# Attention with its tokens in natural order: neighbour values by tokens, the other heads' blocks by stride

## The chip, the cores and the metric

The kernel runs on one core of a Trainium2 chip. The metric is the device time of one execution in microseconds. A core has a matrix engine (TensorE, PE in the profile; PEld is its weight load), a vector engine (VectorE, DVE), an activation engine (ScalarE, ACT), a general engine (GpSimd, POOL) and a queue engine (SyncE, SP). Operands lie in SBUF, 128 partitions wide; matmul results go to PSUM, eight banks of 128 x 512 fp32.

## The reference

Two residual layers over 512 tokens of 1024 features, each a mixer and a SwiGLU block with a norm ahead; layer 0 mixes by causal pooling, layer 1 by attention, and a last norm ends it. The change lies in the attention mixer, which has 16 heads of 64 features in three groups:

```python
ATTN_PATTERNS = ((128, 1), (512, 4), (2048, 16))      # window, dilation
...
qkv = jnp.einsum('bsd,de->bse', h, w_qkv).reshape(B, S, 3, N_HEADS, HEAD_DIM)
q = rope(qkv[:, :, 0]) * HEAD_DIM ** -0.5
k = rope(qkv[:, :, 1])
v = qkv[:, :, 2]
for (window, dilation), n_g in zip(ATTN_PATTERNS, HEAD_GROUPS):    # 6, 5, 5 heads
    o_g, lse_g = dilated_window_attention(q[:, :, sl], k[:, :, sl], v[:, :, sl], window, dilation)
```

The first six heads ("neighbour heads") look at the last 128 tokens, dilation 1: their blocks are 128 consecutive tokens, and a block sees itself and the block before. The other ten ("far heads") have dilations of 4 and 16: a query sees only keys whose token number has the same remainder by 4 (or by 16), so the kernel gives them four blocks by residue, block r holding the tokens 4j + r. The groups' outputs are weighted by a softmax over their log-sum-exps and go through an output projection.

## The kernel before

All products are fp32 by splitting: every operand is a high part rounded for the matrix engine and a low rest, and a product is three matmuls, high-high, high-low and low-high. Weights are loaded by DMA into `wraw`, cast to the high part on ACT (L171), subtracted on DVE for the low part (L175), and kept in a ring of five pairs (`wspl`). `queue` lists them in the order of use; `weights(i)` loads five items ahead and splits four ahead, and its argument `held` counts earlier items that are still in use. TensorE's instructions run in the order in which the program writes them; the other engines' orders are planned from priorities and dependencies, and `high_priority(URGENT)` moves an instruction ahead.

The operand of attention, `h`, is the normed and turned stream: features on partitions, tokens along the row, in a high and a low part. Before the change its 512 tokens stand in residue order: first the tokens 0, 4, 8, ..., then 1, 5, 9, ... The transposed blocks are spread into that order as they leave PSUM (`by_residue`, L390), a block of 128 tokens going to four runs of 32; the first three projections, made in two halves so that they can begin before all tokens are there (`by_halves`, L1142), take four runs of 64 from it.

The attention stage then goes in steps. Eight pairs of query and key projections, 24 matmuls of 512 columns each (L264 to L266), are each followed by the rotary embedding (`rope`, L1011: a shuffle and a product on DVE, a product on GpSimd, a sum on DVE). For the far heads' five tiles the sum is plain (L1020). For the neighbour heads' three tiles it restores the token order: queries go out at a stride of four elements (L1025), keys come from runs of 32 (L1022), so that within a block of 128 the keys stand by residue; the masks (`_constants`) and the values follow that order. `later(step)` runs the scores of earlier heads between the projections: near scores for a neighbour pair, far scores for a far one, then the softening (mask and maximum on DVE, exponential on ACT) and the turning of the probabilities by rows (`turn_by_rows`, L366).

Values come next, in steps 16 to 26. The neighbour heads' 384 value columns are made by features: three projections of 128 columns each with the tokens moving (L1278); ACT copies each result into `vt` with the key order (L1283); four transposes on TensorE turn it (L1273), one step later, and ACT copies it to `v` (L1274). The far heads' 640 columns are made by tokens, in two parts of 320 (L1287 to L1309): a block of 128 tokens of `h` is the weight operand, the value weights move, and four banks hold the four blocks while the eight chunks of features are summed. Between the pieces `between(step)` calls `later`, and at steps 19, 21 and 23 the groups' sums, their weights and the spreading of these weights by small DMAs. Far scores of the last four heads come at step 17.

There are four banks for these products (`mm`), and four more for scores and turned probabilities (`psc`, `ptr`). Products of probabilities and values (`merged`, L1321) and the output projection follow, in natural token order.

The functions that the change touches:

Of the kernel before, what the change touches and what calls it, by code (L numbers as in the profile page):

```python
# [10 lines left out]
F32 = mybir.dt.float32  # L11
# [6 lines left out]
P = 128  # L18
S = 512
# [48 lines left out]


PLAN = _plan()  # L70
TOKENS = np.arange(S).reshape(J, R).T.reshape(-1)
BY_GROUP = [6, 7, 4, 5, 2, 3, 0, 1]


# [1 line left out]
def trunk_kernel(ctx: ExitStack, tc: tile.TileContext, x_in, xT, gam, gains, consts, ident_d, w0, wT, w1, wv, w_down, out):  # L76
# [45 lines left out]
    def enqueue(src, shape, kind="w", **more):  # L122
        queue.append(dict(kind=kind, src=[src], shape=shape, **more))
        return len(queue) - 1
# [128 lines left out]

    j_ffn = [enqueue_ffn(0)]
    j_qk = [enqueue(w0[10 + i], (8, P)) for i in range(16)]
    j_v0 = [enqueue(w0[26 + i], (8, P)) for i in range(3)]
    j_v = []
    for at in (0, VB):
        j_v.append([enqueue(wv[:, 8 * at + c * 2 * VB : 8 * at + (c + 1) * 2 * VB], (2, VB)) for c in range(4)])
    j_wo = [wo(2 * i, 0) for i in range(4)] + [wo(2 * i, 1, pool="b") for i in range(4)]  # L260
    j_ffn.append(enqueue_ffn(1))

# [124 lines left out]
        cast = nc.scalar.copy(hi, src)  # L387
        return cast, (eng or nc.vector).tensor_sub(lo, src, hi.bitcast(F32))

    def by_residue(b):  # L390

        n = P // R

        def places(h, half, tp):
            at = h[:, 4 * half : 4 * half + 4, :].rearrange("p c (r j) -> p c r j", r=R)
            return at[:, :, :, b * n : (b + 1) * n], tp.rearrange("p c (i r) -> p c r i", r=R)

        return places

    def turned(norm, shift, b, tps, order):  # L400

        hi, lo = tokens_at(shift)
        for half, tp in enumerate(tps):
            norm.turn(b, half, tp)
        for half, tp in enumerate(tps):
            (to_hi, src), (to_lo, _) = order(hi, half, tp), order(lo, half, tp)
            with tc.high_priority(URGENT):
                split(to_hi, to_lo, src)
# [199 lines left out]
    def ffn(layer, norm, third, nxt):  # L608
# [8 lines left out]
        with ExitStack() as fctx:  # L617
# [322 lines left out]
                    nc.scalar.dma_start(rows[:, COLS[1]], t[:, COLS[1]])  # L940

            ready_block = emit if final else norm.prepare
            turn_block = lambda b, pair: turned(norm, 0, b, [by_four(pair[:, n, :]) for n in range(2)], by_residue(b))

            every = PLAN[-1][3]
            last.product(5, every)
# [39 lines left out]
    with ExitStack() as actx:  # L986
# [17 lines left out]
        ap.tile([P, 8], F32, name="gap3")  # L1004
        state = {}

        def blocks_of(a):

            return a.rearrange("p (r b i) -> p b r i", r=R, b=4)

        def rope(ps, t, name):  # L1011
            a = aw.tile([P, S], F32, name="ropea")
            sw = aw.tile([P, S], F32, name="ropeb")
            nc.vector.stream_shuffle(sw, ps, PARTNER)
            nc.vector.tensor_mul(a, ps, cosr)
            nc.gpsimd.tensor_mul(sw, sw, sinr)
            out = aw.tile([P, S], F32, name=name, bufs=3)

            if t >= 3:
                nc.vector.tensor_add(out, a, sw)  # L1020
            elif name == "k":
                nc.vector.tensor_add(out.rearrange("p (b r i) -> p b r i", b=4, r=R), blocks_of(a), blocks_of(sw))  # L1022
            else:
                by_r = lambda z: z.rearrange("p (r j) -> p r j", r=R)
                nc.vector.tensor_add(out.rearrange("p (j r) -> p r j", r=R), by_r(a), by_r(sw))  # L1025
            return out

        def slot(h, i):
# [108 lines left out]
                    turn_by_rows(by_rows.pop(0), ("ACT", "DVE"), bank)  # L1137

        h_hi, h_lo = tokens_at(0)
        late = lambda b, pool, name: turned(norm, 0, b, [pool.tile([P, 4, P], F32, name=name) for _ in range(2)], by_residue(b))  # L1140

        def by_halves(js):  # L1142

            n = J // 2
            part = lambda z, i: z.rearrange("p (r j) -> p r j", r=R)[:, :, i * n : (i + 1) * n]
            got = [(mm.tile([P, S], F32, name="mm"), weights(j, held=i)) for i, j in enumerate(js)]
            for i in (1, 0):
                for at, (ps, (whi, wlo)) in enumerate(got):
                    if i == 1 and at == 2:
                        late(1, psc, "sc")  # L1150
                    for c in range(NC):
                        if (i, at, c) == (1, 1, NC // 2):
                            late(0, ptr, "tp")
                        mm3(part(ps, i), whi[:, c, :], wlo[:, c, :], part(h_hi[:, c, :], i), part(h_lo[:, c, :], i),
                            i == 1 and c == 0, c == NC - 1, skip_group_check=True)
            return [ps for ps, _ in got]
# [106 lines left out]
                    spread_weights()  # L1263


        to_turn = []

        def turn():
            m, vt = to_turn.pop(0)

            tp = (mm.tile() if m == 0 else psc_bank()).rearrange("p (b d) -> p b d", b=4)
            for b in range(4):
                nc.tensor.transpose(tp[:, b, :], vt[:, b * P : (b + 1) * P], ident)  # L1273
            nc.scalar.copy(v[:, :, m * P : (m + 1) * P], tp)  # L1274

        step = 16
        for m in range(3):
            ps = project(j_v0[m], h_hi, h_lo)  # L1278
            if to_turn:
                turn()  # L1280
            vt = aw.tile([P, S], F32, name="ropea")
            with tc.high_priority(URGENT):
                nc.scalar.copy(vt.rearrange("p (b r i) -> p b r i", b=4, r=R), blocks_of(ps))  # L1283
            to_turn.append((m, vt))
            between(step)
            step += 1
        for part in range(2):  # L1287
            at = VA + part * VB
            pv = [mm.tile([P, S], F32, name="mm") for _ in range(4)]
            for c in range(4):  # L1290
                whi, wlo = weights(j_v[part][c])
                for b in range(4):
                    for kk in range(2):
                        kc = 2 * c + kk
                        o = pv[b][:, :VB]
                        xh, xl = (z[:, kc, b * P : (b + 1) * P] for z in (h_hi, h_lo))
                        nc.tensor.matmul(o, lhsT=xh, rhs=whi[:, kk, :], start=kc == 0, stop=False)  # L1297
                        nc.tensor.matmul(o, lhsT=xh, rhs=wlo[:, kk, :], start=False, stop=False)  # L1298
                        nc.tensor.matmul(o, lhsT=xl, rhs=whi[:, kk, :], start=False, stop=kc == NC - 1)  # L1299
                    if c == 3:  # L1300
                        with tc.high_priority(URGENT):
                            if b // 2:
                                copied = nc.vector.tensor_copy(v[:, b, at : at + VB], pv[b][:, :VB])
                            else:
                                nc.scalar.copy(v[:, b, at : at + VB], pv[b][:, :VB])
                if to_turn:
                    turn()
                between(step, copied)
                step += 1  # L1309
        assert not pend_sc and not by_rows  # L1310
# [53 lines left out]
def _constants():  # L1364

    s, d = np.arange(P)[:, None], np.arange(SPAN)[None, :]
    bands = []
    for first in (True, False):
        for w in WINDOWS:
            inside = (s <= d) & (s > d - w)  # L1370
            count = np.minimum(d + 1, w) if first else w
            bands.append(np.where(inside, np.float32(1.0) / np.float32(count), np.float32(0.0)) - (s == d).astype(np.float32))
    freq = (np.float32(1.0) / np.float32(10000.0) ** (np.arange(0, HD, 2, dtype=np.float32) / np.float32(HD))).astype(np.float32)
    ang = (np.arange(S, dtype=np.float32)[None, :] * freq[:, None]).astype(np.float32)
    cos = np.cos(ang.astype(np.float64))
    sin = np.sin(ang.astype(np.float64))
    cos = np.tile(np.concatenate([cos, cos], 0)[ROPE_ORDER], (2, 1))[:, TOKENS]
    sin = np.tile(np.concatenate([-sin, sin], 0)[ROPE_ORDER], (2, 1))[:, TOKENS]
    q = np.arange(P)[:, None]
    k = np.arange(P)[None, :]  # L1380
    key = R * (k % 32) + k // 32
    near = np.where(key <= q, 0.0, NEG)
    prev = np.where(key >= q, 0.0, NEG)
    own = np.where(k <= q, 0.0, NEG)
    comb = np.where((k <= q) & (k % 4 == q % 4), 0.0, NEG)
    parts = bands + [cos, sin, near, prev, near, own, comb]
    return np.ascontiguousarray(np.concatenate(parts, 1).astype(np.float32))
# [8 lines left out]
def _layout(x, norm_mix, norm_ffn, norm_final, pool_w_in, pool_w_group, pool_scale, pool_w_out,  # L1396
# [6 lines left out]
    qkv = attn_w_qkv[0]  # L1403
    rot = lambda w: w.reshape(D, H, HD)[:, :, ROPE_ORDER].reshape(D, D)
    qk = np.stack([_tiles(rot(qkv[:, :D]), 8), _tiles(rot(qkv[:, D : 2 * D]), 8)], 1).reshape(16, P, 1024)
    w0 = np.concatenate([w_in, grp, qk, _tiles(qkv[:, 2 * D :], 8)[:3]], 0)
    gu = [np.stack([_tiles(ffn_w_gate[i], NF), _tiles(ffn_w_up[i], NF)], 1).reshape(2 * NF, P, 1024) for i in range(2)]
    wv = qkv[:, 2 * D :].reshape(NC, P, D).transpose(1, 0, 2)
    wv = np.concatenate([wv[:, :, a:b].reshape(P, -1) for a, b in ((VA, VA + VB), (VA + VB, D))], 1)
    return dict(  # L1410
        x_in=x[0], xT=x[0].T, gam=gam, gains=gains, consts=_constants(), ident=np.eye(P, dtype=np.float32),
        w0=w0, wT=np.stack([pool_w_out[0], attn_w_out[0]]), w1=np.concatenate(gu, 0), wv=wv,
# [16 lines left out]
```

## Time and profile before

| what | value |
|---|---|
| median of 3 runs | 981.48 us (980.54 to 981.59) |
| profiled execution, its own time | 980.24 us |
| its span, first to last instruction | 978.5 us |
| TensorE's granted clock, mean | 0.999 |
| matmuls | 6028 |
| values stage, from its first projection to the last block's product | 542.5 to 593 us from the span's start |

How to read it: a busy share says how long an engine had something in flight. Matmuls are pipelined, so the recorded length of one is longer than the distance to the next one's start, and a TensorE that is busy for 99% may still lose time between starts. The chain of waits follows the last instruction back through what released each step. The timeline lists an engine's instructions with start and length. In groups of instructions, "128x320 f32 x64 | 20.1, 314" means 64 instructions of that shape, 20.1 us busy, 314 ns each on the mean.

### The profile page before, as it was taken

How to read it: one execution, taken by the hardware profiler on the slowest of the kernel's cores; microseconds unless marked ns; L12 is line 12 of the kernel's file. 1: busy time of each engine (PE TensorE's matmuls, PEld its weight loads, DVE VectorE, ACT ScalarE, POOL GpSimd, SP SyncE). 2: the span in 40 equal slices, each digit the busy share in tenths (PEclk: the TensorE clock that was granted, in tenths of full speed). 3: DMA queues.
4: the chain of work that ended last, by engine and by line, in shares of the span. 5: the costliest groups of instructions: out<-in, count | busy, mean ns of one | idle time of the engine just before them, and what ended most of it. 6: DMA issues, size and time to landing. Idle time of an engine off the chain costs nothing.

```text
span 978.5 us, 15597 instructions
## 1 busy us (share of the span) xinstructions
PE 970.9 (99%) x6028; PEld 862.6 (88%) x6028; DVE 783.9 (80%) x1083; ACT 575.3 (59%) x903; POOL 124.7 (13%) x124
## 2 busy tenths in 40 slices
PE   9999999999999999999999999999999999999997
PEld 8888899988988999889888899899998998899886
DVE  6475799888888888797897547579988898888876
ACT  6573566655665666574553554366664675567655
POOL 0002010010011111101212124101011101110110
PEclk9999999999999999999999999999999999999999
DMA  9448267479668877555221249627657947987652
GB/s 346 176 157 207 45 187 186 124 200 248 165 151 222 218 201 159 117 193 165 86 79 55 62 137 295 115 59 204 174 145 205 251 111 173 250 213 193 153 134 101
DMA packets 79466, 163.00 MB, mean 167 GB/s; under 512 B 6096, under 2 KB 6480, under 8 KB 79392
## 3 DMA queue, kind: packets, MB, share of 16 engines
q1 hardware_dynamic: 58544, 122.04, 37.6%
q0 software_dynamic: 20560, 39.69, 23.7%
q8 instruction: 47, 0.77, 0.3%
q14 instruction: 27, 0.22, 0.1%
q10 hardware_dynamic: 288, 0.27, 0.1%
HBM read 159.85 MB, written 2.13 MB: 166 GB/s over the span
## 4 chain that ended last, share of the span: by engine, by line
PE 99%; ACT 0%; DVE 0%; issue 0%; ACTq 0%
PE pair L703 32%; PE pair L847 21%; PE p L729 5%; PE mm L264 5%; PE mm L266 4%; PE mm L265 4%; PE pair L729 4%; PE r L729 2%; PE early L515 2%; PE mm L425 2%; PE mm L427 2%; PE mm L426 2%; PE mm L729 1%; PE mm L1297 1%; PE mm L1298 1%; PE mm L1299 1%
## 5 line engine op out<-in xcount | busy, mean ns | idle before, releaser
L175 DVE TENSOR_TENSOR wlo<-wraw,whi 128x1024 fp32r<-128x1024 f32 (+2 forms) x190 | 221.7, 1172 | 65.6 <-ACT whi L171 65.0
L171 ACT CAST whi<-wraw 128x1024 fp32r<-128x1024 f32 (+2 forms) x189 | 184.0, 979 | 138.4 <-PE pair L703 27.8
L171 ACT CAST whi<-vraw 128x1024 fp32r<-128x1024 f32 (+1 forms) x108 | 105.2, 980 | 117.6 <-DVE vraw L177 39.8
L175 DVE TENSOR_TENSOR wlo<-vraw,whi 128x1024 fp32r<-128x1024 f32 (+1 forms) x108 | 121.5, 1133 | 46.2 <-ACT whi L171 46.2
L703 PE MATMUL pair<-h,whi 128*128 128x512 f32 (+1 forms) x640 | 143.2, 349 | 0.0
L703 PEld LDWEIGHTS pair<-h,whi 128*128 128x128 f32 x640 | 109.1, 188 | 13.4
L703 PE MATMUL pair<-t,whi 128*128 128x512 f32 (+1 forms) x512 | 110.6, 337 | 0.0
L847 PE MATMUL pair<-whi,u_hi 128*128 128x512 f32 (+1 forms) x284 | 109.9, 387 | 0.0
L847 PE MATMUL pair<-wlo,u_hi 128*128 128x512 f32 (+1 forms) x284 | 109.9, 387 | 0.0
L847 PE MATMUL pair<-whi,u_lo 128*128 128x512 f32 (+1 forms) x284 | 109.7, 386 | 0.0
L703 PEld LDWEIGHTS pair<-t,whi 128*128 128x128 f32 x512 | 86.1, 190 | 8.4
L703 PE MATMUL pair<-h,wlo 128*128 128x256 f32 x512 | 89.2, 281 | 0.0
L703 PEld LDWEIGHTS pair<-h,wlo 128*128 128x128 f32 x512 | 76.1, 188 | 4.2
L138 POOL DMA_DIRECT2D wraw<-w x22 | 26.6, 1211 | 396.0 <-DMA wraw<-w 123.2
L177 DVE TENSOR_TENSOR vraw<-vraw,wraw 128x1024 f32<-128x1024 f32 (+1 forms) x66 | 75.2, 1139 | 0.7
L703 PE MATMUL pair<-t,wlo 128*128 128x256 f32 x384 | 71.9, 282 | 0.0
L264 PE MATMUL mm<-h,whi 128*128 128x512 f32 (+1 forms) x176 | 64.3, 365 | 0.0
L266 PE MATMUL mm<-h,wlo 128*128 128x512 f32 (+1 forms) x176 | 63.4, 360 | 0.0
L265 PE MATMUL mm<-h,whi 128*128 128x512 f32 (+1 forms) x176 | 63.4, 360 | 0.0
L847 PEld LDWEIGHTS pair<-whi,u_lo 128*128 128x128 f32 x284 | 53.3, 188 | 10.9
L847 PEld LDWEIGHTS pair<-whi,u_hi 128*128 128x128 f32 x284 | 53.4, 188 | 10.4
L847 PEld LDWEIGHTS pair<-wlo,u_hi 128*128 128x128 f32 x284 | 53.4, 188 | 10.2
(363 smaller groups left out, 2021.4 us busy)
## 6 DMA issues: line engine op xcount, KB each, us to landing
wraw<-w SPq DMA_DIRECT2D x116, 512.0 KB, 4.7
wraw<-w_down SPq DMA_DIRECT2D x32, 512.0 KB, 4.2
vraw<-w SPq DMA_DIRECT2D x22, 512.0 KB, 4.8
wraw<-w POOLq DMA_DIRECT2D x22, 512.0 KB, 6.9
vraw<-w POOLq DMA_DIRECT2D x22, 512.0 KB, 9.1
wraw<-wT SPq DMA_DIRECT2D x16, 512.0 KB, 4.4
vraw<-w_down POOLq DMA_DIRECT2D x12, 512.0 KB, 6.5
wraw<-w_down SPq DMA_DIRECT2D x24, 256.0 KB, 3.3
```

What stands on the lines that cost most here:

```text
L138: nc.gpsimd.dma_start(dst, more, accum_op=ALU.add)
L171: nc.scalar.copy(hi[:, :n], raw[:, :n])
L175: nc.vector.tensor_sub(lo[:, :n], raw[:, :n], hi[:, :n].bitcast(F32))
L177: nc.vector.tensor_add(raws[into][:, :n], raws[into][:, :n], raws[more][:, :n])
L264: nc.tensor.matmul(ps, lhsT=whi, rhs=xhi, start=first, stop=False, **kw)
L265: nc.tensor.matmul(ps, lhsT=whi, rhs=xlo, start=False, stop=False, **kw)
L266: nc.tensor.matmul(ps, lhsT=wlo, rhs=xhi, start=False, stop=last, **kw)
L425: nc.tensor.matmul(ps, lhsT=xhi, rhs=w[0][:, k, :], start=first, stop=False)
L426: nc.tensor.matmul(ps, lhsT=xhi, rhs=w[1][:, k, :], start=False, stop=False)
L703: mat = lambda o, w, m, **kw: nc.tensor.matmul(o, lhsT=w, rhs=m, skip_group_check=True, **kw)
L729: nc.tensor.matmul(ps[:, g, :], lhsT=w[:, g, c, :], rhs=right[:, z, c, :], start=i in (0, 1, 3) and g + c + k == 0, stop=c == 3 and k == 2 ...
L847: nc.tensor.matmul(acc(t), lhsT=u, rhs=w, start=first, stop=n == len(places) - 1, skip_group_check=True)
```

## The change

The tokens of `h` stay in natural order. Transposed blocks leave PSUM without reordering, and the halves of the first projections are plain slices. The rotary tables and the masks follow. The rotary sum is now plain for the neighbour heads' tiles, and for the far heads' five pairs it reads both operands at a stride of four elements and writes the residue order.

The neighbour heads' values are made by tokens like the others: 384 columns, in two rounds of two blocks each, from four pieces of weights of two feature chunks, all four held through both rounds. Step 16 follows the third piece of round one, step 17 (with the last far scores) the first piece of round two, and step 18 the end of round two. The far heads' value products keep their shape, but their weight operand is now every fourth token of `h` (`by_residue` in the new form), 128 elements at a stride of 16 bytes. The projections, the scratch copies, the transposes and the copies behind them are gone, and the value weights of the neighbour heads move from `w0` to `wv`.

```diff
-    def by_residue(b):
-
-        n = P // R
+    def in_order(b):
 
         def places(h, half, tp):
-            at = h[:, 4 * half : 4 * half + 4, :].rearrange("p c (r j) -> p c r j", r=R)
-            return at[:, :, :, b * n : (b + 1) * n], tp.rearrange("p c (i r) -> p c r i", r=R)
+            return h[:, 4 * half : 4 * half + 4, b * P : (b + 1) * P], tp
...
-    j_v0 = [enqueue(w0[26 + i], (8, P)) for i in range(3)]
     j_v = []
-    for at in (0, VB):
-        j_v.append([enqueue(wv[:, 8 * at + c * 2 * VB : 8 * at + (c + 1) * 2 * VB], (2, VB)) for c in range(4)])
+    for at, n in ((0, VA), (VA, VB), (VA + VB, VB)):
+        j_v.append([enqueue(wv[:, 8 * at + c * 2 * n : 8 * at + (c + 1) * 2 * n], (2, n)) for c in range(4)])
...
-            if t >= 3:
+            if t < 3:
                 nc.vector.tensor_add(out, a, sw)
-            elif name == "k":
-                nc.vector.tensor_add(out.rearrange("p (b r i) -> p b r i", b=4, r=R), blocks_of(a), blocks_of(sw))
             else:
-                by_r = lambda z: z.rearrange("p (r j) -> p r j", r=R)
-                nc.vector.tensor_add(out.rearrange("p (j r) -> p r j", r=R), by_r(a), by_r(sw))
+                by_r = lambda z: z.rearrange("p (j r) -> p r j", r=R)
+                nc.vector.tensor_add(out.rearrange("p (r j) -> p r j", r=R), by_r(a), by_r(sw))
...
-            n = J // 2
-            part = lambda z, i: z.rearrange("p (r j) -> p r j", r=R)[:, :, i * n : (i + 1) * n]
+            part = lambda z, i: z[:, HALVES[i]]
...
+        def values(pv, blocks, at, n, c, w, tokens):
+
+            whi, wlo = w
+            for b, ps in zip(blocks, pv):
+                o = ps[:, :n]
+                for kk in range(2):
+                    kc = 2 * c + kk
+                    xh, xl = (tokens(z[:, kc, :], b) for z in (h_hi, h_lo))
+                    nc.tensor.matmul(o, lhsT=xh, rhs=whi[:, kk, :], start=kc == 0, stop=False)
+                    nc.tensor.matmul(o, lhsT=xh, rhs=wlo[:, kk, :], start=False, stop=False)
+                    nc.tensor.matmul(o, lhsT=xl, rhs=whi[:, kk, :], start=False, stop=kc == NC - 1)
+                if c == 3:
+                    with tc.high_priority(URGENT):
+                        copy = (nc.scalar.copy, nc.vector.tensor_copy)[b // 2]
+                        copied = copy(v[:, b, at : at + n], o)
+            return c == 3 and copied
+
+        by_block = lambda z, b: z[:, b * P : (b + 1) * P]
+        by_residue = lambda z, r: z.rearrange("p (j r) -> p r j", r=R)[:, r, :]
+        ws = [weights(j, held=i) for i, j in enumerate(j_v[0])]
+        for blocks in ((0, 1), (2, 3)):
+            pv = [mm.tile([P, S], F32, name="mm") for _ in blocks]
+            for c in range(4):
+                values(pv, blocks, 0, VA, c, ws[c], by_block)
+                if (blocks[0], c) in ((0, 2), (2, 0)):
+                    between(16 + blocks[0] // 2)
+        between(18)
+        step = 19
         for part in range(2):
-            at = VA + part * VB
             pv = [mm.tile([P, S], F32, name="mm") for _ in range(4)]
             for c in range(4):
-                whi, wlo = weights(j_v[part][c])
...
+                copied = values(pv, range(4), VA + part * VB, VB, c, weights(j_v[1 + part][c]), by_residue) or copied
                 between(step, copied)
                 step += 1
...
-    key = R * (k % 32) + k // 32
-    near = np.where(key <= q, 0.0, NEG)
-    prev = np.where(key >= q, 0.0, NEG)
+    near = np.where(k <= q, 0.0, NEG)
+    prev = np.where(k >= q, 0.0, NEG)
```

More of the change, by code (lines that the diff above doesn't have):

```diff
@@ L70 @@
 PLAN = _plan()
-TOKENS = np.arange(S).reshape(J, R).T.reshape(-1)
 BY_GROUP = [6, 7, 4, 5, 2, 3, 0, 1]
@@ L942, in ffn @@
             ready_block = emit if final else norm.prepare
-            turn_block = lambda b, pair: turned(norm, 0, b, [by_four(pair[:, n, :]) for n in range(2)], by_residue(b))
+            turn_block = lambda b, pair: turned(norm, 0, b, [by_four(pair[:, n, :]) for n in range(2)], in_order(b))
             every = PLAN[-1][3]
@@ L1005, in trunk_kernel @@
         state = {}
-        def blocks_of(a):
-            return a.rearrange("p (r b i) -> p b r i", r=R, b=4)
         def rope(ps, t, name):
@@ L1139, in trunk_kernel @@
         h_hi, h_lo = tokens_at(0)
-        late = lambda b, pool, name: turned(norm, 0, b, [pool.tile([P, 4, P], F32, name=name) for _ in range(2)], by_residue(b))
+        late = lambda b, pool, name: turned(norm, 0, b, [pool.tile([P, 4, P], F32, name=name) for _ in range(2)], in_order(b))
         def by_halves(js):
-            n = J // 2
-            part = lambda z, i: z.rearrange("p (r j) -> p r j", r=R)[:, :, i * n : (i + 1) * n]
+            part = lambda z, i: z[:, HALVES[i]]
             got = [(mm.tile([P, S], F32, name="mm"), weights(j, held=i)) for i, j in enumerate(js)]
@@ L1263, in between @@
                     spread_weights()
[L1266 to L1286, printed above, removed]
+        def values(pv, blocks, at, n, c, w, tokens):
[13 more added lines that the diff above has]
+            return c == 3 and copied
@@ L1287, in trunk_kernel @@
+        between(18)
+        step = 19
         for part in range(2):
-            at = VA + part * VB
             pv = [mm.tile([P, S], F32, name="mm") for _ in range(4)]
             for c in range(4):
-                whi, wlo = weights(j_v[part][c])
[L1292 to L1307, printed above, removed]
@@ L1376, in _constants @@
     sin = np.sin(ang.astype(np.float64))
-    cos = np.tile(np.concatenate([cos, cos], 0)[ROPE_ORDER], (2, 1))[:, TOKENS]
-    sin = np.tile(np.concatenate([-sin, sin], 0)[ROPE_ORDER], (2, 1))[:, TOKENS]
+    cos = np.tile(np.concatenate([cos, cos], 0)[ROPE_ORDER], (2, 1))
+    sin = np.tile(np.concatenate([-sin, sin], 0)[ROPE_ORDER], (2, 1))
     q = np.arange(P)[:, None]
     k = np.arange(P)[None, :]
-    key = R * (k % 32) + k // 32
-    near = np.where(key <= q, 0.0, NEG)
-    prev = np.where(key >= q, 0.0, NEG)
+    near = np.where(k <= q, 0.0, NEG)
+    prev = np.where(k >= q, 0.0, NEG)
     own = np.where(k <= q, 0.0, NEG)
@@ L1405, in _layout @@
     qk = np.stack([_tiles(rot(qkv[:, :D]), 8), _tiles(rot(qkv[:, D : 2 * D]), 8)], 1).reshape(16, P, 1024)
-    w0 = np.concatenate([w_in, grp, qk, _tiles(qkv[:, 2 * D :], 8)[:3]], 0)
+    w0 = np.concatenate([w_in, grp, qk], 0)
     gu = [np.stack([_tiles(ffn_w_gate[i], NF), _tiles(ffn_w_up[i], NF)], 1).reshape(2 * NF, P, 1024) for i in range(2)]
     wv = qkv[:, 2 * D :].reshape(NC, P, D).transpose(1, 0, 2)
-    wv = np.concatenate([wv[:, :, a:b].reshape(P, -1) for a, b in ((VA, VA + VB), (VA + VB, D))], 1)
+    wv = np.concatenate([wv[:, :, a:b].reshape(P, -1) for a, b in ((0, VA), (VA, VA + VB), (VA + VB, D))], 1)
     return dict(
```

## The prediction

> **What bounds the kernel now.** I read the page's totals and its chain of waits first, then the list of who waited for whom on TensorE, then TensorE's timeline through the stage that the change rewrites.
>
> ```profile
> span 978.5 us, 15597 instructions
> PE 970.9 (99%) x6028; PEld 862.6 (88%) x6028; DVE 783.9 (80%) x1083; ACT 575.3 (59%) x903; POOL 124.7 (13%) x124
> ...
> PE 99%; ACT 0%; DVE 0%; issue 0%; ACTq 0%
> ```
>
> ```profile
> PE mm L302 <- DVE odd_rows L296: 1.1, 1, 1.1
> ```
>
> TensorE is 99% of the chain that ended last, and the only wait that the second list charges to its matmuls is 1.1 us at the very start. So work taken from ACT, DVE, POOL or a DMA queue is worth nothing by itself. A change here is worth what it does to the beat at which TensorE starts matmuls, plus any wait that it creates. A matmul's recorded length (0.39 us) overlaps the next ones; what counts is the distance between starts, so I take starts from the timeline.
>
> ```profile
> 542.46 0.39 PE L264 MATMUL mm<-h,whi 128*128 128x512 f32 x1
> ...
> 553.12 0.40 PE L266 MATMUL mm<-h,wlo 128*128 128x512 f32 x1
> 553.35 0.60 PE L1273 MATMUL mm<-ident,ropea 128*128 128x128 f32 x4
> 553.88 0.71 PE L366 MATMUL tp<-ident,e 64*128 64x64 f32 x16
> ...
> 556.86 0.50 PE L264 MATMUL mm<-h,whi 128*128 128x512 f32 x1
> ...
> 562.21 0.39 PE L266 MATMUL mm<-h,wlo 128*128 128x512 f32 x1
> 562.44 0.60 PE L1273 MATMUL sc<-ident,ropea 128*128 128x128 f32 x4
> 562.79 0.39 PE L1297 MATMUL mm<-whi,h 128*128 128x320 f32 x1
> 563.03 0.31 PE L1298 MATMUL mm<-wlo,h 128*128 128x320 f32 x1
> ...
> 566.25 0.31 PE L1299 MATMUL mm<-whi,h 128*128 128x320 f32 x1
> ...
> 566.98 0.30 PE L1298 MATMUL mm<-wlo,h 128*128 128x320 f32 x1
> ```
>
> From the first row to the second TensorE issues two whole projections, 48 matmuls of 512 columns and so 47 steps: (553.12 - 542.46) / 47 = 0.2268 us. From 563.03 to 566.25 it issues 23 matmuls of 320 columns, 22 steps: 0.1464 us. The two give a straight line: (0.2268 - 0.1464) / 192 = 0.419 ns a column and 12 ns on top. A matmul of 384 columns therefore steps by 0.1464 + 64 x 0.000419 = 0.1732 us.
>
> **The change part by part.**
>
> *Neighbour heads' values.* Removed: 3 projections of 24 matmuls, 72 x 0.2268 = 16.33 us, and three turns of four transposes. A turn costs what it pushes back. The second: from 562.21 to 562.79, where a matmul without it would start 0.227 later, is 0.35 more, and the step after it is 0.24 in place of 0.146, another 0.09: 0.44 us. The third, 566.25 to 566.98 in place of two steps of 0.146, is 0.44 too. The first (553.35 to 553.88, 0.53) stands ahead of row transposes that would themselves pay 0.09 of the change-over: 0.44. Together 1.32 us. Added: 4 blocks x 8 chunks x 3 = 96 matmuls of 384 columns, 96 x 0.1732 = 16.63 us. Net: 16.63 - 16.33 - 1.32 = **-1.02 us**.
>
> *Copies.* Three ACT copies into a reordered scratch and three behind the transposes go; two ACT and two DVE copies of 128x384 come.
>
> ```profile
> L1283 ACT COPY ropea<-mm 128x512 f32<-128x512 f32 x3 | 1.7, 574 | 0.0
> L1305 ACT COPY v<-mm 128x320 f32<-128x320 f32 x4 | 1.6, 425 | 0.2 <-PE mm L1299 0.2
> L1303 DVE COPY v<-mm 128x320 f32<-128x320 f32 x4 | 1.9, 485 | 0.0
> ```
>
> By columns the new ones take about 425 + 64 x (574 - 425) / 192 = 475 ns on ACT and some 550 ns on DVE. They pay only where TensorE wants their bank, so this is a question of four banks. Round one fills two, round two the other two; the far scores, which come after the first quarter of round two, take round one's two banks; the next part takes all four.
>
> ```profile
> 553.36 0.72 ACT L171 CAST whi<-wraw 128x640 fp32r<-128x640 f32 x1 [4.23 <-issue]
> ```
>
> Round one runs from 542.46 for 48 x 0.1732 = 8.3 to 550.8, inside a stretch in which ACT sat idle 4.23 us (549.1 to 553.36), so its copies are done by 551.9. The far scores come at 550.8 + 12 x 0.173 = 552.9: free by a microsecond. Round two ends at about 562.2 (552.9, plus 3.1 us for the scores and row transposes, which now run from 553.88 to 556.86 with 0.1 for the change-over, plus 36 x 0.173). Its first bank had its last matmul at 561.0 and is wanted at 562.2; end of that matmul and copy need 0.33 + 0.55 us. What DVE does then:
>
> ```profile
> 555.58 1.29 DVE L1090 SCALAR_TENSOR_TENSOR e<-sc,gain 128x512 f32<-128x512 f32 x2 [0.63 <-PE sc L1080]
> ...
> 566.05 0.20 DVE L1194 TENSOR_TENSOR mx<-mx,near 128x24 f32<-128x24 f32 x1 [4.24 <-ACT mx L1193]
> ```
>
> Masking these scores keeps DVE busy until 4.24 us before 566.05, so to 561.8; after the change that ends one microsecond earlier, and the gap behind it stays. Cover 0.3 us; with one such 0.68 us operation ahead of the copy, TensorE would wait up to 0.5 us. I take 0 (0 to +0.5).
>
> *Weights.* Four pieces of 768 columns replace three of 1024: the same bytes on SP's queue, loaded as far ahead. All four are held until round two is through, so the splits of the next part's second to fourth piece wait for a slot, the second to 552.9 + 2.1. It is used only at 565.7, and ACT is idle before 553.36. The third becomes free at 558, under the 7 us of exponentials, and may wait for their end:
>
> ```profile
> 565.20 0.19 ACT L1036 ACTIVATION_READ_ACCUMULATOR e<-e,neg 128x1 f32 x1
> ```
>
> 565.4 + 0.72 for the high part + 0.83 for the low one is 567.0, wanted at 569.2. Cost 0; without these 2 us of cover TensorE would wait for each microsecond of lateness.
>
> *Rotary sums and masks.* The last addition of the six neighbour tensors becomes plain; that of the ten others reads both operands at a stride of 16 bytes. Whether such a read costs is also the question of the next part, so here are the rows.
>
> ```profile
> L1020 DVE TENSOR_TENSOR q<-ropea,ropeb 128x512 f32<-128x512 f32 x5 | 3.4, 685 | 0.9 <-POOL ropeb L1016 0.9
> L1025 DVE TENSOR_TENSOR q<-ropea,ropeb 128x512 f32<-128x512 f32 x3 | 3.4, 1121 | 0.9 <-POOL ropeb L1016 0.9
> L388 DVE TENSOR_TENSOR h<-pair,h 128x512 fp32r<-128x512 f32 x4 | 2.6, 682 | 0.0
> L1233 DVE TENSOR_TENSOR den<-den,mx 128x24 f32<-128x24 f32 x1 | 0.2, 182 | 2.6 <-DMA mx<-gw 2.6
> L1194 DVE TENSOR_TENSOR mx<-mx,near 128x24 f32<-128x24 f32 x1 | 0.2, 204 | 4.2 <-ACT mx L1193 4.2
> L1218 DVE RECIPROCAL gtop<-gtop 128x4 f32<-128x4 f32 x1 | 0.2, 178 | 0.0
> L1219 DVE RECIPROCAL den<-near 128x24 f32<-128x24 f32 x1 | 0.3, 295 | 0.0
> L1220 DVE RECIPROCAL den<-den 128x40 f32<-128x40 f32 x1 | 0.4, 391 | 0.0
> ```
>
> A stride-16 write (L1025) takes 1121 in place of 685 ns. A stride-16 read of PSUM (L388) takes nothing extra. A read of SBUF with a stride of 32 bytes (L1194) takes 22 ns more on 24 elements than L1233's packed one, 0.9 ns each, about one DVE beat (685 ns for 512 elements is at most 1.3 ns each). Yet L1219 reads the same strided tile and lies on the line of the packed L1218 and L1220: 178 + 20 x (391 - 178) / 36 = 296. An operation that takes an element only every 5.9 ns doesn't feel the stride. So the ten sums cost DVE between 0 and 0.44 us each; they are used a projection (5.4 us) or more later, and no TensorE wait stands behind them. Cost 0.
>
> *Other heads' blocks by stride.* [...] What a packed load costs shows where the moving side is short:
>
> ```profile
> 39.08 3.97 PE early L562 x36
> ```
>
> These band products move 144 columns or fewer, worth 12 + 60 = 72 ns, but step by 3.97 / 36 = 0.110 us: there the load of 128 columns sets the beat, 0.86 ns a column, twice as long as a moving column takes (0.419). At 320 columns the beat is 0.1464, so a load may grow by a third before it shows. Bounds: below 0 (nothing in it gets shorter); above, the load grows by DVE's 0.9 ns a column, to 0.225 us, and costs 192 x (0.225 - 0.146) = +15 us. The two sides of the DVE rows decide differently: the fast operation pays a second beat, the slow one doesn't. [...] I take 0, with little confidence, and keep +15 for the range.
>
> [...]
>
> *The rest.* `h` and the first three projections' halves are now packed where they went in four pieces of 64.
>
> ```profile
> L266 PE MATMUL mm<-h,wlo 128*128 128x256 f32 x48 | 13.6, 283 | 0.0
> L703 PE MATMUL pair<-h,wlo 128*128 128x256 f32 x512 | 89.2, 281 | 0.0
> ```
>
> The pieces last 283 ns against 281 for packed operands of that size: at most 144 x 0.002 = 0.3 us to gain; I take 0. The score steps, the sums and the spreading of the groups' shares keep their places between the same products and all move 0.6 to 1 us earlier together with TensorE.
>
> **Sum:** 980.24 us for the profiled execution (span 978.5), less 1.02: 979.2. That execution was 1.24 below the median of the timed runs, 981.48; at the median the forecast is **980.5**, its own range 979.2 to 981.5.
>
> **Rivals.**
>
> *Strided weight loads set the beat* (slower). Place: the 192 products of the ten other heads. It decides from a load of 0.146 us on. [...] For it: L1025 and L1194 show that DVE pays for such strides; 99% of TensorE's time is on the chain, so all of it would show. Against it: L1219, and the slack of a third. Time 980.5 + 13 to 14 = 994, down to 987.
>
> *A bank arrives late.* The waits named above, 0.5 us at the start of the next part and as much where the far scores take round one's banks if ACT's copies slip behind a cast, eat the gain: 981.5. Against it: the 4.23 and 4.24 us of idle time.
>
> *More than forecast.* TensorE would have to lose 2 us. Only 1.32 us of turns are there to lose, and 0.3 from packed halves; the rest would be chance between runs, 980.54 to 981.59 before. Time 979.3.
>
> **How the numbers follow.** Forecast 0.52, strided loads 0.38, late bank 0.05, more gain 0.05. About 0.2% (2.0 us) is what a measurement can tell from no change: faster means below 979.5, slower above 983.4. The strided loads give slower 0.38; the forecast and the late bank lie within, except for a few per cent of the forecast that runs low: same 0.53, faster 0.09. The range must reach the rival: 979.2 to 995.5, which leaves out about 0.15, a load dearer than 0.225 and a gain beyond 1.3 us.
>
> **What would show it.** L1273 and its copies are gone. Products of 384 columns step by 0.173 us, and no TensorE wait is listed beyond the one at the start. The decisive row is the step of the 320-column products: 0.146 if I am right, 0.18 to 0.225 if the rival is. The ten rotary sums show 685 or about 1100 ns, which tells what DVE pays for such a read. A wait of TensorE for an ACT or DVE copy of `v` would be the bank rival.

## The result and the profile after

The changed kernel takes 995.6 us (median of 4 runs, 995.45 to 995.96) where the kernel before takes 981.01 (4 runs, 980.38 to 981.59) beside it: a ratio of 1.0149, with a 95% interval of 1.0132 to 1.0167. It is slower by 14.6 us. The forecast was 980.5; its range ended at 995.5, and the outcome lies 1.6 us above where the first rival, strided weight loads, put it (994).

The page of the changed kernel, its totals and the chain that ended last (profiled execution 995.52 us):

```profile
span 993.7 us, 15623 instructions
PE 986.3 (99%) x6040; PEld 881.3 (89%) x6040; DVE 787.6 (79%) x1086; ACT 574.1 (58%) x900; POOL 124.7 (13%) x124
...
PE 99%; ACT 0%; DVE 0%; issue 0%; ACTq 0%
```

The list of what TensorE's matmuls waited for, changed kernel (what waited, for what; us in total, times, longest):

```profile
PE mm L300 <- DVE odd_rows L294: 1.1, 1, 1.1
```

The span grew by 993.7 - 978.5 = 15.2 us, and neither view shows where: TensorE is still 99% of the chain and waits for nobody but at the start (1.1 us). Matmuls that are slower by themselves would be in neither. So the starts in TensorE's timeline come next, changed kernel (start, recorded length, instruction):

```profile
542.23 0.33 PE L1262 MATMUL mm<-whi,h 128*128 128x384 f32 x1
...
552.48 0.34 PE L1264 MATMUL mm<-whi,h 128*128 128x384 f32 x1
...
562.07 0.37 PE L1262 MATMUL mm<-whi,h 128*128 128x320 f32 x1
562.28 0.40 PE L1263 MATMUL mm<-wlo,h 128*128 128x320 f32 x1
...
573.02 0.40 PE L1264 MATMUL mm<-whi,h 128*128 128x320 f32 x1
```

From the first row to the second there are 60 matmuls of 384 columns, 59 steps: 10.25 / 59 = 0.1737 us, as forecast. From 562.07 to 573.02 there are 48 of 320 columns, 47 steps: 10.95 / 47 = 0.2330 us in place of 0.1464. With 192 such matmuls this is 192 x (0.2330 - 0.1464) = 16.6 us, more than the whole growth. Most of the missing 1.4 us is the gain of the neighbour part and of the stretch before it: the first far product starts at 562.07 where it started at 562.79 (0.23 of these 0.72 us were there before the first value product, which starts at 542.23 where it started at 542.46), and the third turn of four transposes (0.44 us), which stood behind it, is gone; together 1.2 us.

### The profile page after: what moved, and what is told of

Same layout as the page of the kernel before. It is cut to its first block, busy times and chain, and to the rows that moved or that the text cites. A ratio compares the mean times of both kernels' runs of the same rounds, so it can differ in the third digit from the quotient of the medians.

```text
span 993.7 us, 15623 instructions
## 1 busy us (share of the span) xinstructions
PE 986.3 (99%) x6040; PEld 881.3 (89%) x6040; DVE 787.6 (79%) x1086; ACT 574.1 (58%) x900; POOL 124.7 (13%) x124
## 4 chain that ended last, share of the span: by engine, by line
PE 99%; ACT 0%; DVE 0%; issue 0%; ACTq 0%
PE pair L698 32%; PE pair L842 21%; PE p L724 5%; PE pair L724 4%; PE mm L262 4%; PE mm L264 4%; PE mm L263 4%; PE r L724 2%; PE mm L420 2%; PE early L510 2%; PE mm L422 2%; PE mm L421 2%; PE mm L1262 2%; PE mm L1264 2%; PE mm L1263 2%; PE mm L724 1%
## 5 line engine op out<-in xcount | busy, mean ns | idle before, releaser
L174 DVE TENSOR_TENSOR wlo<-wraw,whi 128x1024 fp32r<-128x1024 f32 (+3 forms) x191 | 221.8, 1166 | 83.1 <-ACT whi L170 82.4
L170 ACT CAST whi<-wraw 128x1024 fp32r<-128x1024 f32 (+3 forms) x190 | 184.1, 975 | 151.7 <-PE pair L698 24.7
L698 PEld LDWEIGHTS pair<-t,wlo 128*128 128x128 f32 x384 | 59.4, 190 | 2.5
L262 PE MATMUL mm<-h,whi 128*128 128x512 f32 (+1 forms) x152 | 54.8, 361 | 0.0
L264 PE MATMUL mm<-h,wlo 128*128 128x512 f32 (+1 forms) x152 | 54.1, 356 | 0.0
```

The lines of the kernel that those rows point to most:

```text
L170: nc.scalar.copy(hi[:, :n], raw[:, :n])
L174: nc.vector.tensor_sub(lo[:, :n], raw[:, :n], hi[:, :n].bitcast(F32))
L262: nc.tensor.matmul(ps, lhsT=whi, rhs=xhi, start=first, stop=False, **kw)
L264: nc.tensor.matmul(ps, lhsT=wlo, rhs=xhi, start=False, stop=last, **kw)
L698: mat = lambda o, w, m, **kw: nc.tensor.matmul(o, lhsT=w, rhs=m, skip_group_check=True, **kw)
```

## The experiments

**The stride alone.** In the kernel before, the far heads' blocks are read at a stride of four elements; nothing else is changed.

```diff
-                        xh, xl = (z[:, kc, b * P : (b + 1) * P] for z in (h_hi, h_lo))
+                        xh, xl = (z[:, kc, :].rearrange("p (j r) -> p r j", r=R)[:, b, :] for z in (h_hi, h_lo))
```

> The kernel before, with one thing of the change: the weight operand of the 192 far value products is every fourth token of h (h is still in residue order, so the far heads get the values of other tokens). Theories 1 and 2: the step goes from 0.146 to 0.233 us, 192 x 0.087 = 16.7 us more, 997.7. Theory 3: no change, 981.

Measured: 996.79 us (4 runs, 996.41 to 996.97) against 980.49, ratio 1.0165 (1.0149 to 1.018). Weight loads of these products grouped by line, first the kernel before, then this one (count, busy us, mean ns):

```profile
L1298 PEld LDWEIGHTS mm<-wlo,h 128*128 128x128 f32 x64 | 12.0, 188 | 0.0
```

```profile
L1298 PEld LDWEIGHTS mm<-wlo,h 128*128 128x128 f32 x64 | 21.1, 329 | 0.0
```

Same line, same shape, same count; only the stride differs, and the recorded load goes from 188 to 329 ns. The stride alone makes the whole loss: 16.3 us, against 16.6 worked out from the steps above.

**The change without the stride.** The changed kernel, with the far blocks packed.

```diff
-        by_residue = lambda z, r: z.rearrange("p (j r) -> p r j", r=R)[:, r, :]
+        by_residue = by_block
```

> The changed kernel, but the weight operand of the far heads' 192 value products is the packed block of 128 tokens in place of every fourth token (so the far heads get the values of other tokens; everything else is computed). Theory 1, the strided weight load sets the beat: the step of the 320-column products is back from 0.233 to 0.146 us, 16.7 us go, and the rest of the change shows alone, about 980.0 us against 981.0 before (1 us less). Theory 2, the strided load collides with the moving operand: the same here. Theory 3, something else in the new order (held weights, rounds, banks) slows these products: the step stays at 0.233 and the time near 995.

Measured: 983.8 us (5 runs, 982.9 to 984.77) against 980.49, ratio 1.0033 (1.002 to 1.0046). The step of the far products is back at 0.1465 us (46 steps from 561.73 to 568.47), so the stride's price is confirmed from the other side. But the neighbour part, forecast at -1.0, stands at +3.3. Waits of TensorE in this kernel that the changed kernel doesn't have, and its timeline around the long one:

```profile
PE tp L1229 <- DVE den L1221: 3.0, 1, 3.0
...
PE mm L1262 <- DVE v L1268: 0.2, 1, 0.2
```

```profile
581.17 0.31 PE L1264 MATMUL mm<-whi,h 128*128 128x320 f32 x1
584.45 0.27 PE L1229 MATMUL tp<-ident,den 128*64 128x128 f32 x1 [2.96 <-DVE den L1221]
...
585.65 0.47 PE L1262 MATMUL mm<-whi,h 128*128 128x320 f32 x1
...
588.05 0.47 PE L1262 MATMUL mm<-whi,h 128*128 128x320 f32 x1
```

The transpose of the heads' denominators, which carry the groups' shares, comes 3.28 us after the matmul ahead of it in place of 0.15. From 585.1 us on, for some 3.4 us, the step is (588.05 - 585.65) / 9 = 0.267 in place of 0.146: the granted clock fell (0.91 on the mean of 581 to 586 us and 0.74 on that of 586 to 591, with 1.00 on the 5 us before and after), which costs some 13 x 0.12 = 1.6 us more. TensorE came there one microsecond earlier, so 3.1 + 1.6 - 1.0 = 3.7, near the difference of the spans, 982.0 - 978.5 = 3.5. What TensorE waits for is a chain of short steps on DVE with two small DMA rounds (`mx<-near` and `mx<-gw`) between them. DVE's timeline before, and then in this kernel:

```profile
573.38 0.17 DVE L1206 COPY gain<-mx 128x8 f32<-128x8 f32 x1 [4.97 <-DMA mx<-near]
...
575.57 0.27 DVE L1233 TENSOR_TENSOR den<-den,gw 128x20 f32<-128x20 f32 x2
...
582.03 0.18 DVE L1233 TENSOR_TENSOR den<-den,mx 128x24 f32<-128x24 f32 x1 [2.61 <-DMA mx<-gw]
```

```profile
574.25 0.17 DVE L1194 COPY gain<-mx 128x8 f32<-128x8 f32 x1 [6.47 <-DMA mx<-near]
...
574.93 0.82 DVE L174 TENSOR_TENSOR wlo<-wraw,whi 128x640 fp32r<-128x640 f32 x1
575.67 0.68 DVE L1104 COPY pT<-tp 128x512 f32<-128x512 f32 x1
576.27 0.68 DVE L1104 COPY pT<-sc 128x512 f32<-128x512 f32 x1
576.87 0.29 DVE L1201 SCALAR_TENSOR_TENSOR gw<-gain 128x4 f32<-128x4 f32 x3
...
584.12 0.18 DVE L1221 TENSOR_TENSOR den<-den,mx 128x24 f32<-128x24 f32 x1 [4.31 <-DMA mx<-gw]
```

And TensorE before, at the same transpose:

```profile
582.36 0.27 PE L1241 MATMUL tp<-ident,den 128*64 128x128 f32 x1
```

In the kernel before, the last merge ended at 582.03 + 0.18 = 582.21 and TensorE issued the transpose at 582.36: 0.15 us of slack. Now TensorE comes there one microsecond earlier, the first DMA round lands 0.9 later, and a weight split and two copies of probabilities stand ahead of L1201. In the changed kernel this chain is no earlier (its last merge ends at 586.6), and TensorE doesn't wait for it, because the strided products bring it there only at 591.4.

**Is it DVE's order?** In the two kernels above, the shares are worked out ahead of those copies and of the later splits.

```diff
+                  with tc.issue_after(shares_done[0]) if shares_done and eng == "DVE" else nullcontext():
                     (nc.scalar.copy if eng == "ACT" else nc.vector.tensor_copy)(pT[:, at : at + n, rows], tp[:, :n, :])
...
             if step == 19:
                 group_sums()
-            if step == 21:
-                group_weights()
+                shares_done.append(group_weights().ins)
+                for j in j_v[2][2:]:
+                    queue[j]["behind"] = shares_done[0]
```

With the far blocks packed:

> The packed far products again (values of other tokens), with one more edit: DVE works out the groups' shares before the last copies of turned probabilities and the later splits, the order that it had in the kernel before. In the packed run TensorE stood 3.3 us at the transpose of the shares, which waited for DVE's merge and its DMA, and its clock was halved for some us after that. Theory A, DVE's planned order makes the shares late: the wait goes, the clock stays up, and the time is 1 us below before, about 979.5 to 980 where before takes 980.5. Theory B, the small DMAs are slow by themselves and TensorE only comes too early now: at least 2 of the 3.3 us stay, 982 to 984.

With the far blocks strided, as in the change:

> The changed kernel, strided loads and all, with the same edit of DVE's order. Theory A: TensorE reaches the transpose some 5 us later there and waits for nothing, so the edit changes nothing: 995 to 996. If the late shares cost something in the changed kernel too: 993 or less.

Measured: packed, 981.69 us (11 runs, 981.14 to 985.0) against 980.49, ratio 1.0015 (1.0006 to 1.0024); strided, 995.55 us (4 runs, 995.29 to 996.15), the same as the change. DVE's order (theory A) was 2.1 of the packed kernel's 3.3 us and nothing of the change's 14.6. The packed time fits neither forecast: it lies above theory A's 980 and below theory B's 982. DVE's timeline in the packed one:

```profile
575.90 0.17 DVE L1195 COPY gain<-mx 128x8 f32<-128x8 f32 x1 [7.02 <-DMA mx<-near]
...
581.86 0.18 DVE L1223 TENSOR_TENSOR den<-den,mx 128x24 f32<-128x24 f32 x1
```

The merge ends at 582.04, 2.3 us earlier than without the edit, though the first DMA round lands even later. TensorE does not wait for it: in this profile, which is of the slowest of the 11 runs (985.0), it comes to the transpose only at 583.34, because two banks came late before it. ACT's copies of `v` begin at 578.39 where they began at 576.74 without the edit, and DVE's at 580.94 where they began at 578.92. TensorE's timeline:

```profile
578.88 0.41 PE L1265 MATMUL mm<-whi,h 128*128 128x320 f32 x1 [0.61 <-ACT v L1271]
...
581.48 0.41 PE L1265 MATMUL mm<-whi,h 128*128 128x320 f32 x1 [0.57 <-DVE v L1271]
...
583.34 0.27 PE L1231 MATMUL tp<-ident,den 128*64 128x128 f32 x1
```

These two matmuls start 0.92 and 0.89 us after the one ahead of them in place of 0.15, 1.5 us together: the late bank, a rival of the prediction. The profile has further waits of 0.8 to 1.2 us outside this stage. Whether late banks also make the remaining 1.2 us of the usual run stays open, for the only trace is of the slowest.

**Does the chain have to start earlier?** In the packed kernel, the last far scores, on which the chain rests, come two pieces earlier, with step 16.

```diff
-                if (blocks[0], c) in ((0, 2), (2, 0)):
-                    between(16 + blocks[0] // 2)
+                if (blocks[0], c) == (0, 2):
+                    between(16)
+                    between(17)
```

> The packed far products again (values of other tokens), with one edit: the last far scores run after the third piece of round one in place of the first piece of round two, some 4 us earlier. They begin the chain of the groups' shares (exponentials, sums, two rounds of small DMAs, the merge that the transpose waits for), which in the kernel before ended 0.15 us ahead of that transpose. Theory C, this chain runs beside TensorE with no slack left, so that 1 us saved on TensorE's own path is waited away: with the chain 3 to 4 us earlier the waits go and the microsecond shows, 979.5 where before takes 980.5. If the saving itself isn't there (the change-overs cost less than counted): 980.5 or more, with no wait of TensorE in this stage.

Measured: 979.59 us (11 runs, 978.82 to 981.6) against 980.48 (15 runs), ratio 0.9994 (0.9985 to 1.0003). DVE's timeline and TensorE's:

```profile
570.74 0.17 DVE L1194 COPY gain<-mx 128x8 f32<-128x8 f32 x1 [3.10 <-DMA mx<-near]
...
579.87 0.18 DVE L1221 TENSOR_TENSOR den<-den,mx 128x24 f32<-128x24 f32 x1 [1.47 <-DMA mx<-gw]
```

```profile
581.08 0.31 PE L1264 MATMUL mm<-whi,h 128*128 128x320 f32 x1
581.23 0.27 PE L1229 MATMUL tp<-ident,den 128*64 128x128 f32 x1
```

The merge is through 1.2 us before the transpose, which follows its matmul by one step, and the 3.3 us are gone. The median is 0.9 us below the kernel before, near the forecast 1.0 for the neighbour part; the interval of the ratio takes in no change, so that gain is supported and not shown. What is shown is that the chain had no slack to give (theory C).

**What does the load cost: an addition to each matmul, or a beat of its own?** Three kernels change the number of columns moved. Theory 1 says that the step is the longer of the load and the columns; theory 2 that the stride adds the same 0.087 us to any matmul. First, far blocks packed and the neighbour rounds of 384 columns strided:

```diff
-                values(pv, blocks, 0, VA, c, ws[c], by_block)
+                values(pv, blocks, 0, VA, c, ws[c], by_stride)
```

> The packed far products of the run before last, and the stride of four elements on the weight operand of the 96 neighbour products of 384 columns instead (values of other tokens). Theory 1, the load takes 0.233 us whatever moves: their step goes from 0.173 to 0.233, 96 x 0.060 = 5.8 us above the packed run. Theory 2, the stride adds a fixed 0.087 to each step: 0.260, 8.3 us above it.

Second, in the kernel before, the projections of 512 columns with every fourth element as their weights:

```diff
-            mm3(ps, whi[:, k, :], wlo[:, k, :], hi[:, k, :], lo[:, k, :], k == 0, k == NC - 1)
+            fourth = lambda z: z[:, 4 * (k // 4) : 4 * (k // 4) + 4, :].rearrange("p k (m s) -> p s (k m)", s=4)[:, k % 4, :]
+            mm3(ps, fourth(whi), fourth(wlo), hi[:, k, :], lo[:, k, :], k == 0, k == NC - 1)
```

> The kernel before, with the weights of 13 query and key projections (312 matmuls that move 512 columns) read at a stride of four elements from their pieces (other weights in other places, so queries and keys differ). Theory 1: the load of 0.233 us nearly fits behind the 0.227 that the columns take; step 0.233, 2 us more in all, 983. Theory 2: 0.227 + 0.087 = 0.314, 27 us more, 1008.

One run each: 986.62 us (384 columns) and 984.32 (512 columns) against 980.49. TensorE's timelines, 384 columns and then 512:

```profile
543.07 0.40 PE L1263 MATMUL mm<-wlo,h 128*128 128x384 f32 x1
...
556.61 0.39 PE L1264 MATMUL mm<-whi,h 128*128 128x384 f32 x1
```

```profile
541.78 0.39 PE L266 MATMUL mm<-h,wlo 128*128 128x512 f32 x1
...
545.30 0.40 PE L266 MATMUL mm<-h,wlo 128*128 128x512 f32 x1
```

58 steps make 13.54 / 58 = 0.2334 us, and 15 steps 3.52 / 15 = 0.2347, where theory 2 had 0.260 and 0.314. Theory 1 holds: the step is 0.233 us with 320 and with 384 columns, and with 512 (0.2268 packed, 0.2347 here) the load all but disappears. The edit reaches 16 projections of 24 matmuls, 384 in all (312 for queries and keys, 72 for the neighbour values): 384 x 0.008 = 3.0 of the 3.8 us, and this run's list of waits has 0.7 and 0.2 us that the kernel before lacks.

The time of the 384-column kernel missed the forecast: it is 2.8 us above the packed kernel's, where theory 1 had 5.8. TensorE comes to the transpose of the shares some 6 us later in it, and its wait there is shorter:

```profile
588.83 0.27 PE L1229 MATMUL tp<-ident,den 128*64 128x128 f32 x1 [1.25 <-DVE den L1221]
```

That is 1.7 us less than the 2.96 of the packed kernel, and the step behind it is (591.73 - 589.09) / 18 = 0.147 us, with none of the packed kernel's 0.267, which saves the 1.6 us of the slow steps: 5.8 - 1.7 - 1.6 = 2.5.

**How does the load depend on the stride?** The far products are cut in halves of 160 columns (0.079 us by the line of the prediction), so that the load sets the beat, and the stride is 1, 2, 3, 4 or 8 elements.

```diff
-                    nc.tensor.matmul(o, lhsT=xh, rhs=whi[:, kk, :], start=kc == 0, stop=False)
...
+                    for at_c in range(0, n, n if n == VA else n // 2):
+                        cs = slice(at_c, at_c + (n if n == VA else n // 2))
+                        nc.tensor.matmul(o[:, cs], lhsT=xh, rhs=whi[:, kk, cs], start=kc == 0 and at_c == 0, stop=False, skip_group_check=True)
...
```

> What the load itself costs, laid bare: the changed kernel with each far product cut into two of 160 columns (384 matmuls), so that the columns take only 0.08 us, and the weight operand packed (values of other tokens). Theory 1, the load sets the beat: step 0.110 us as in the band products of before. If the columns set it: 0.079.

> [...]

> [...]

> The same halves, weight operand at the stride of four elements of the change, its own tokens, so only the cut differs from the changed kernel. Theory 1: 0.233 us a step, the same for 160 columns as for 320, so the 384 products take 384 x 0.233 = 89.6 us, 44.8 more than in the changed kernel: about 1040. Theory 2: 0.110 + 0.087 = 0.197, 75.6 us: about 1026.

> The same halves of 160 columns, weight operand at a stride of eight elements, 32 bytes, across two chunks (other values). [...] If the price grows with the distance: well above, 0.110 + 7 x 0.041 = 0.397.

TensorE's timeline in the five kernels, strides 1, 2, 3, 4 and 8, each in a stretch at full granted clock:

```profile
590.19 0.32 PE L1264 MATMUL mm<-whi,h 128*128 128x160 f32 x1
...
606.21 0.27 PE L1266 MATMUL mm<-whi,h 128*128 128x160 f32 x1
```

```profile
591.83 0.33 PE L1264 MATMUL mm<-whi,h 128*128 128x160 f32 x1
...
608.90 0.28 PE L1266 MATMUL mm<-whi,h 128*128 128x160 f32 x1
```

```profile
563.59 0.33 PE L1264 MATMUL mm<-whi,h 128*128 128x160 f32 x1
...
574.13 0.34 PE L1264 MATMUL mm<-whi,h 128*128 128x160 f32 x1
```

```profile
562.43 0.40 PE L1265 MATMUL mm<-wlo,h 128*128 128x160 f32 x1
...
565.93 0.40 PE L1265 MATMUL mm<-wlo,h 128*128 128x160 f32 x1
```

```profile
562.11 0.40 PE L1265 MATMUL mm<-wlo,h 128*128 128x160 f32 x1
...
565.71 0.40 PE L1265 MATMUL mm<-wlo,h 128*128 128x160 f32 x1
```

| stride | steps between the rows | step, us | step / 128 columns, ns | time of one run, us |
|---|---|---|---|---|
| 1 | 143 | 0.1120 | 0.88 | 997.86 |
| 2 (8 bytes) | 143 | 0.1194 | 0.93 | 996.14 |
| 3 (12 bytes) | 60 | 0.1757 | 1.37 | 1032.25 |
| 4 (16 bytes) | 15 | 0.2333 | 1.82 | 1043.75 |
| 8 (32 bytes) | 15 | 0.2400 | 1.88 | 1046.0 |

At stride 4 the steps carry the time: most of the 384 halves ran at 0.235, and 384 x 0.235 - 192 x 0.1464 = 62.1 us, of 62.6 measured against 981.18. The times of strides 1 and 2 stand the other way round from their steps: the run of stride 1 has a wait of 2.5 us in another part of the kernel (for `h`, L386), which the other run lacks. The step doesn't grow evenly with the distance: 0.041 us for each further element, as the expectation for stride 8 has it, would give 0.151 at stride 2, 0.192 at stride 3 and 0.397 at stride 8, against 0.1194, 0.1757 and 0.2400 measured. From 4 to 8 bytes it grows by 0.007 us, from 8 to 12 by 0.056, from 12 to 16 by 0.058, and from 16 to 32 again by 0.007. Why it does so is not shown.

**The moving side.** In the kernel before, the projections' 512 moving tokens are read every fourth element.

```diff
+            by_r = lambda z: z[:, k, :].rearrange("p (j r) -> p r j", r=R)
-            mm3(ps, whi[:, k, :], wlo[:, k, :], hi[:, k, :], lo[:, k, :], k == 0, k == NC - 1)
+            mm3(ps, whi[:, k, :], wlo[:, k, :], by_r(hi), by_r(lo), k == 0, k == NC - 1)
```

> The kernel before, with the stride on the other operand: 13 query and key projections (312 matmuls of 512 columns) move every fourth element of h in place of packed rows (tokens in another order, so queries and keys differ). [...] If it only doubles its 0.42 ns: 0.43, 64 us more, 1045. If the moving port hides it: no change, 981.

One run: 1069.53 us against 980.3. TensorE's timeline:

```profile
566.27 0.64 PE L266 MATMUL mm<-h,wlo 128*128 128x512 f32 x1
...
571.80 0.64 PE L266 MATMUL mm<-h,wlo 128*128 128x512 f32 x1
```

12 steps make 5.53 / 12 = 0.461 us in place of 0.2268: a moving column at this stride costs 0.90 ns, twice its packed 0.44, and half of the 1.82 that the load pays for a column at the same stride. 384 x 0.234 = 89.9 us is the whole difference. The nearest forecast, 1045, had the doubling right; it counted 312 matmuls, without the 72 of the neighbour values, and took 0.43 us a step.

The packed kernels above compute other values than the reference. One way to keep the far blocks packed and compute it would be a second copy of `h` in residue order, whole (512 tokens x 8 chunks x 4 bytes, high and low: 32 KB a partition) or in a smaller ring of copies. Neither was tried, so what it would cost is not shown; its whole prize would be the 0.9 us above.

## Why the prediction was wrong, point by point

- **Neighbour heads' values, -1.02: right in its parts; the gain as a whole is supported and not shown.** The step was 0.1737 (forecast 0.1732) and the turns are gone. From the first value product to the first far one the changed kernel takes 0.49 us less, where the forecast was 0.58 (1.02 without the third turn, which stood behind that product). It pays only where the shares are in time: +3.3 us without, and -0.9, an interval that takes in no change, with the scores moved.
- **Copies and weights, 0: right for the changed kernel.** No wait of TensorE for `v` or for a weight is listed there. But its slow far products leave the copies more time than the forecast did; where these products run at the forecast beat, banks did come late, 0.2 us in the packed kernel and twice 0.6 in the slowest run with the shares first. The copies of the changed kernel by their groups:

```profile
L1268 DVE COPY v<-mm 128x384 f32<-128x384 f32 x2 | 1.1, 556 | 1.0 <-PE mm L1264 1.0
L1268 ACT COPY v<-mm 128x384 f32<-128x384 f32 x2 | 1.0, 479 | 7.3 <-PE mm L1264 7.3
```

- **Rotary sums, 0 (up to 0.44 us each on DVE): right.** They pay nearly the upper bound, and it is hidden. The strided and the plain sum of the changed kernel:

```profile
L1014 DVE TENSOR_TENSOR q<-ropea,ropeb 128x512 f32<-128x512 f32 x5 | 5.4, 1083 | 0.9 <-POOL ropeb L1007 0.9
L1011 DVE TENSOR_TENSOR q<-ropea,ropeb 128x512 f32<-128x512 f32 x3 | 2.0, 683 | 0.9 <-POOL ropeb L1007 0.9
```

- **Other heads' blocks by stride, 0 (up to +15): wrong, and this decides the result.** The step that failed is the one from DVE's slow operation to the weight load: it took the price of a stride for one that a slow reader hides. That was the author's estimate; the 0 supposes a load that a stride of 16 bytes costs nothing, which no run shows, and the recorded load went from 188 to 329 ns. The runs show that the slower reader pays more: 1.82 ns a column at the load, 0.90 at the moving side, each about twice that side's own packed price (0.88 and 0.44). The row that carried the argument, the reciprocal L1219, was no witness: an operation that takes an element only every 5.9 ns says nothing of a load that takes one every 0.86. L1025 (1121 ns in place of 685) and L1194 (204 in place of 182), rows that do pay, were nearer. The slack was read rightly: the runs fit a step that is the longer of load and columns (0.233 with 160, 320 and 384 columns, 0.2347 with 512), and by that a load could have grown to 0.146 unseen.
- **The size of the rival.** Its bound took DVE's 0.9 ns a column on top of 0.86, for a load of 0.225 and +15; the load is 0.233. No run shows the terms behind its 13 to 14 us and its 987; in their place the runs showed 0.233 us, 2.08 times the packed 0.112, and so 16.6 us. With the measured load the prediction's own sum gives 979.2 + 16.6 = 995.8 for the profiled execution, which took 995.52. The range's upper end fell short by 0.1 us.
- **"The score steps, the sums and the spreading of the groups' shares keep their places between the same products and all move 0.6 to 1 us earlier together with TensorE": wrong, but hidden in the result.** The scores keep their place; the chain behind them, with its two DMA rounds, doesn't move with TensorE. It had 0.15 us of slack, which the rows at 582.03 and 582.36 of the kernel before show, and the prediction left it out. Had the stride been free, this would have made the change 3.3 us slower all the same.
- **A bank arrives late, more gain: neither came in the changed kernel.** The first shows in two of the packed ones, as said above.

## What to carry to other kernels

A weight operand read at 16 or 32 bytes from column to column loaded in 0.233 or 0.240 us per 128 fp32 columns in place of 0.112: compare this with the time of the columns moved, and leave such strides to products of about 512 columns, where the step went from 0.2268 to 0.2347 only. The list of waits of the changed kernel has nothing of it; look at the distance between starts. And before work ahead of a chain with DMAs is shortened, look up how much slack the chain's last step has: TensorE that comes early may pay for the gap and then for the clock, 3.1 and 1.6 us in the packed kernel.

## What was not expected of the hardware

The granted clock fell behind one gap, and also where there was none. After the one long wait of the packed kernel (2.96 us idle, 3.28 from start to start) it was 0.74 on the mean of 586 to 591 us, and the steps from 585.14 to 588.58 took 0.25 to 0.27 us in place of 0.146; after the wait of 1.25 us in the 384-column kernel the step stayed at 0.147. In the three kernels of 160-column matmuls with strides of 12, 16 and 32 bytes the clock fell to 0.50 (600 to 640 us), and none of their lists has a wait of TensorE in this stage. The kernel with 16 bytes, busy time by stretches (stretch, length, busy of PE, PEld, DVE, ACT and POOL, granted clock, DMA share, GB/s):

```profile
560.00:566.00 6.00, 6.00 (x32) 6.00 (x30) 3.29 (x8) 6.00 (x26) 0.00 (x0) 1.00 0.00 0
...
600.00:640.00 40.00, 40.00 (x173) 40.00 (x172) 9.47 (x10) 8.14 (x10) 5.73 (x11) 0.50 0.45 133
```

There the columns take about 0.079 of each 0.233 us, a third; in the changed kernel, with 0.146 of 0.233, the mean clock stayed at 0.998, and with packed loads in halves (0.079 of 0.112) it was 1.00 from 585 to 600 us. That the share of time with columns moving decides is the author's estimate from these cases, not shown. At a clock of 0.50 the 16-byte load takes about as long as before (0.235 us from 620.70 to 654.27, 143 steps), while the 12-byte one goes from 0.176 to 0.214 (613.39 to 643.96, 143 steps); why the two differ stays open.
